# The norms ahead of a product, without GpSimd: a hybrid transformer trunk on one core

## The chip, the cores and the metric

The kernel runs on one core of a Trainium2 chip. Five engines work in parallel, each through its own list of instructions in order: TensorE (PE in the profile, with its weight loads as PEld), VectorE (DVE), ScalarE (ACT), GpSimd (POOL) and SyncE (SP), which here only issues DMAs. The metric is the device time of one execution in microseconds; the median of three runs is 3382.01 us.

## The reference

The program is a two-layer trunk over 1024 latent tokens and 256 context tokens, 1024 channels wide, in f32. Every sub-layer begins with the same step, an RMS norm with a scale and a shift that depend on a conditioning vector, ahead of a matrix product:

```
def rms_norm(x, gain=None):
    y = x32 * lax.rsqrt(jnp.mean(x32 * x32, axis=-1, keepdims=True) + EPS)
...
hx = rms_norm(x) * (1.0 + sc1) + sh1
...
x = x + g1 * mx
x = x + g2 * sq_relu_mlp(rms_norm(x) * (1.0 + sc2) + sh2, w_mlp_in[l], w_mlp_out[l])
```

Layer 0 mixes with an mLSTM and a Hyena convolution side by side, layer 1 with neighbourhood attention over the latent tokens and all context keys. Each mixer has an output product with a gated residual, and each layer ends with a squared-ReLU MLP of width 4096 (the last layer for the latent tokens alone).

## The kernel before

Channels lie on the 128 partitions, in eight blocks of 128, and tokens along the free dimension, in three groups: 512 and 512 latent tokens and 256 context tokens (`GR`). Every f32 product is made of three matmuls on halves: an operand is split into a rounded `hi` and a rest `lo`, and `gemm` adds `hi*hi`, `hi*lo` and `lo*hi` in PSUM (L177 to L179) for each of the eight channel blocks.

A norm has two parts. `norm_sum` squares the eight blocks on ScalarE (L250) into tiles `n`, adds them up, and lets a matmul with a matrix of ones (L266) sum over the partitions, so that each partition holds the sum over all channels. There are two ways to add. With `pre=False`, used for the first norms of the program, the eight squares go through TensorE one after the other. With `pre=True`, used by `norm_group`, they are added in pairs and then as a tree, and one matmul sums the result. After that, `rstd_from` makes the inverse root `r` on ScalarE and VectorE.

`norm_apply` then makes the two halves of the normalised input, block by block. On the usual path VectorE makes `xn = x * (1 + scale) * r`, ScalarE adds the shift and writes the rounded half `hi` (L289), and VectorE writes `lo = xn + shift - hi`. For a block `k` in `ONPOOL` the path is another: GpSimd makes `x * r` into a tile `s`, ScalarE makes `hi` from it (L283) and the unrounded value in place (L284), and GpSimd subtracts them. Two-input instructions of all engines are recorded at the helpers' lines: L96 for a plain `tensor_tensor`, L108 for `scalar_tensor_tensor`.

The tiles come from rings: four buffers under the tag `n2` (shown as `n`; squares, the steps of the inverse root, `r` itself and the usual path's `xn`) and four under `s2` (shown as `s`; partial sums and the GpSimd path's `xn`). A tile that needs a buffer waits for the last reader of the one before.

`norm_group` is called eight times: three groups ahead of the first MLP, where the norm of a group is written behind the residual products of the next one (`LATE2 = 1`); three groups at the end of the first MLP, for the attention's projections; and two groups ahead of the last MLP, between output products of the attention. Six of these have 512 columns and two have 256. Around them, VectorE also takes matmul results out of PSUM into the residual stream (L108), and splits weights (`wl`, L113); ScalarE makes the rounded half of the weights (`wh`, L112).

The order of each engine's list isn't the order of the source. A planner (the Tile framework's scheduler) takes instructions by priority and by its own durations, gives out the buffers, and writes the lists; `pr(...)` raises the priority of some parts.

Of the kernel before, what the change touches and what calls it, by code (L numbers as in the profile page):

```python
# [12 lines left out]
ALU = mybir.AluOpType  # L13
# [14 lines left out]
def kernel(ctx: ExitStack, tc: tile.TileContext, A, out):  # L28
    nc = tc.nc
    V, S, T, G = nc.vector, nc.scalar, nc.tensor, nc.gpsimd  # L30
# [29 lines left out]
    def pr(k):  # L60
        k = HP.get(k, k)
        return ExitStack() if k is None else tc.high_priority(k)
    PS3 = dict(g=3, f=3, m=1, n=1)
    LATE2 = 1
    ONPOOL = (1, 4)
    PS0, PS1 = dict(g=2, f=2, m=1, t=2, q=1), dict(g=4, f=3, m=1)
    PS2 = dict(g=3, f=3, m=1, q=1)
    FS, FH, FM = (0, 0, 0), (0, 1, 0, 1, 0, 1, 0, 2), (3, 4, 4)
# [7 lines left out]
    def pt(shape, tag):  # L76
        cnt[0] += 1
        return psp[0].tile(shape, F32, tag=tag, bufs=psp[1][tag], name=f"ps{tag}_{cnt[0]}")
# [7 lines left out]
    def s2(shape=None):  # L86
        return mk(base, shape or [P, 512], "s2", 4)

    def n2(shape=None):
        return mk(base, shape or [P, 512], "n2", 4)  # L90
# [4 lines left out]
    def tt(o, a, b, op, e=None):  # L95
        return (e or V).tensor_tensor(out=o, in0=a, in1=b, op=op)  # L96

    def add(o, a, b):
        return tt(o, a, b, ALU.add)
# [26 lines left out]
    def rstd_from(ps, n, scale, dst, tmp=None):  # L126

        tmp = tmp or s2
        v = tmp()
        S.activation(v[:, :n], ps, AF.Identity, bias=epsc, scale=scale)  # L130
        y = tmp()
        S.activation(y[:, :n], v[:, :n], AF.Ln)
        S.activation(y[:, :n], y[:, :n], AF.Exp, scale=-0.5)
        mul(dst, y[:, :n], y[:, :n])
        stt(v[:, :n], dst, -0.5, v[:, :n], ALU.mult, ALU.mult)
        stt(dst, v[:, :n], 1.5, y[:, :n], ALU.add, ALU.mult)
# [107 lines left out]
    def norm_sum(xk, n, pre, at=None):  # L244

        ps = pt([P, 512], "m")
        acc = []
        for k in range(8):
            sq = n2()
            S.activation(sq[:, :n], xk(k), AF.Square)  # L250
            if not pre:
                T.matmul(ps[:, :n], ones, sq[:, :n], start=(k == 0), stop=(k == 7))
            elif k % 2 == 0:
                acc.append(sq)
            else:
                a = s2()
                tt(a[:, :n], acc.pop()[:, :n], sq[:, :n], ALU.add, (G, V)[k // 2 % 2])
                acc.append(a)
                if k % 4 == 3:
                    b, a = acc.pop(), acc.pop()  # L260
                    add(a[:, :n], a[:, :n], b[:, :n])
                    acc.append(a)
        if pre:
            add(acc[0][:, :n], acc[0][:, :n], acc[1][:, :n])
            with pr(at):
                T.matmul(ps[:, :n], ones, acc[0][:, :n], start=True, stop=True)  # L266
        r = n2()
        rstd_from(ps[:, :n], n, 1.0 / 1024, r[:, :n], n2)
        return r

    def norm_group(xk, n, l, sub_i, which, hi, lo, at=None):

        with pr("ng"):
            norm_apply(norm_sum(xk, n, True, at), xk, n, l, sub_i, which, hi, lo, True)

    def norm_apply(r, xk, n, l, sub_i, which, hi, lo, pre, ks=range(8)):
        sh, sc = sub_i * 24, sub_i * 24 + 8
        for k in ks:
            b, c = modT[l][:, sh + k, which:which + 1], modT[l][:, sc + k, which:which + 1]
            if k in (ONPOOL if pre else ONP0):  # L280
                xn = s2()
# [773 lines left out]
    with tc.tile_pool(name="hp", bufs=1, side="right") as hp:  # L1055
        hc = {}
        stage = lambda: mk(hp, [P, 512], "st", 1)
        with tc.tile_pool(name="mo", bufs=1, side="right") as mo:
# [13 lines left out]
            def between(u):  # L1072
                if u == -1:
                    hc.update(hyena_consts(hp))
                    mod_part(0, 0, mo, ("wm", 3), "q")
                for v in NS:
                    g = NS.index(v)
                    t0, n = GR[g]
                    which = 0 if t0 < LAT else 1
                    if u == v:  # L1080
                        norms[g] = norm_sum(xload(t0, n), n, False), xload(t0, n)
                    if u in (v, v + 0.5):
                        r, x = norms[g]
                        norm_apply(r, x, n, 0, 0, which, h[0][g], h[1][g], False, range(0, 8)[slice(*NA[u - v])])
                if u > 4 and u == int(u):
                    filler(FS[u - 5], stage)
# [281 lines left out]
```

## Time and profile before

| what | us |
| --- | --- |
| runs (three) | 3377.65, 3382.01, 3385.40 |
| the profiled execution | 3372.65 |
| its span, first to last instruction | 3370.9 |
| PE busy in the span | 3239.5 |
| DVE busy | 2050.1 |
| ACT busy | 1211.5 |
| POOL busy | 272.2 |

The span is what the profile covers; the 1.75 us beside it lie ahead of the first and behind the last recorded instruction. Busy time says how long an engine had an instruction in work, and matmuls are recorded as overlapping, so the PE figure isn't the share of its peak. The norms of `norm_group` lie in three stretches of the span: about 920 to 1010 us (first MLP), 1860 to 1945 us (attention) and 2600 to 2690 us (last MLP). In a timeline row stand the start, the duration, the engine, the line, the operation, output and inputs by the program's names, shapes and count; in brackets the engine's idle time ahead of it and what ended it. In a row of a group stand the total busy time and the mean ns of one, and behind the last bar the idle time ahead of them with its releasers.

### The profile page before, as it was taken

To read this page: it belongs to the slowest core of one execution; us is meant where nothing else is said; L and a number is where in the kernel's file an instruction comes from. 1 tells how busy PE (TensorE), PEld (TensorE's weight loads), DVE (VectorE), ACT (ScalarE), POOL (GpSimd) and SP (SyncE) were. 2 spreads that over 40 slices of the span, in tenths; PEclk is the share of its full clock that TensorE was granted. 3 is DMA by queue.
4 is the path that set the end of the run, shared out by engine and by line. 5 is a ranking of instruction groups with operands and counts; after the bars stand their busy time and mean duration, and the time that the engine had idled before them with its cause. 6 is when DMAs were issued, how large, how long until landed. Compare 5 with 4: busy or idle time off the path is not lost.

```text
span 3370.9 us, 45320 instructions
## 1 busy us (share of the span) xinstructions
PE 3239.5 (96%) x18044; PEld 2640.3 (78%) x18044; DVE 2050.1 (61%) x3673; ACT 1211.5 (36%) x2555; POOL 272.2 (8%) x277
## 2 busy tenths in 40 slices
PE   6889999999989999999999999999999899999999
PEld 4778887778868887878888777777777688888887
DVE  4858997556684454444445776766666654555444
ACT  5742221343441211111121576666664421212121
POOL 0320001011120000000000311111110100000000
PEclk8899999999999999999999999999999999999999
DMA  6432224765522212122110222222224111111111
GB/s 212 153 112 67 80 73 156 231 232 199 193 84 90 75 57 94 57 82 69 51 44 32 72 68 63 65 70 66 70 92 148 61 57 50 51 50 45 49 46 69
DMA packets 140878, 306.12 MB, mean 91 GB/s; under 512 B 12497, under 2 KB 74057, under 8 KB 139258
## 3 DMA queue, kind: packets, MB, share of 16 engines
q1 hardware_dynamic: 131018, 266.60, 24.0%
q0 software_dynamic: 6464, 28.84, 2.7%
q10 hardware_dynamic: 3184, 7.78, 0.7%
q8 instruction: 142, 2.33, 0.3%
q14 instruction: 70, 0.57, 0.1%
HBM read 255.93 MB, written 43.05 MB: 89 GB/s over the span
## 4 chain that ended last, share of the span: by engine, by line
PE 61%; DMA 3%; DVE 3%; ACT 2%; issue 1%; POOL 0%; ACTq 0%; DVEq 0%; POOLq 0%
PE psg L177 10%; PE psg L178 10%; PE psg L179 9%; PE psf L312 8%; PE psf L313 8%; PE psf L314 8%; DMA wm<-in_w_mod 2%; PE psf L1014 2%; PE psm L999 1%; PE psf L978 1%; PE psf L979 1%; DVE n L108 1%; PE psf L1018 1%; PE psm L1006 1%; PE psm L218 1%
## 5 line engine op out<-in xcount | busy, mean ns | idle before, releaser
L177 PE MATMUL psg<-h,wh 128*128 128x512 f32 (+1 forms) x2728 | 1015.2, 372 | 17.5 <-ACT h L289 8.4
L179 PE MATMUL psg<-h,wl 128*128 128x512 f32 (+1 forms) x2728 | 1005.6, 369 | 11.6 <-DVE big L585 5.9
L178 PE MATMUL psg<-h,wh 128*128 128x512 f32 (+1 forms) x2728 | 1012.0, 371 | 3.5 <-DVE h L108 2.6
L177 PEld LDWEIGHTS psg<-h,wh 128*128 128x128 f32 x2728 | 517.0, 190 | 112.0 <-issue 15.9
L179 PEld LDWEIGHTS psg<-h,wl 128*128 128x128 f32 x2728 | 517.1, 190 | 101.4 <-issue 10.8
L178 PEld LDWEIGHTS psg<-h,wh 128*128 128x128 f32 x2728 | 517.4, 190 | 98.0 <-issue 13.6
L108 DVE SCALAR_TENSOR_TENSOR x<-psf,modT,x 128x512 f32<-128x512 f32 (+1 forms) x512 | 347.2, 683 | 222.6 <-PE psf L314 222.3
L313 PE MATMUL psf<-al,w2h 128*128 128x512 f32 (+1 forms) x1280 | 471.8, 369 | 0.3 <-DVE al L113 0.3
L314 PE MATMUL psf<-ah,w2l 128*128 128x512 f32 (+1 forms) x1280 | 471.3, 368 | 0.0
L312 PE MATMUL psf<-ah,w2h 128*128 128x512 f32 (+1 forms) x1280 | 470.0, 370 | 1.2 <-ACT ah L112 1.0
L112 ACT CAST w2h<-w2r 128x1024 fp32r<-128x1024 f32 x64 | 67.3, 1051 | 766.5 <-PE psf L313 594.4
L312 PEld LDWEIGHTS psf<-ah,w2h 128*128 128x128 f32 x1280 | 241.3, 189 | 45.3 <-ACT ah L112 3.9
L313 PEld LDWEIGHTS psf<-al,w2h 128*128 128x128 f32 x1280 | 241.5, 189 | 41.8 <-DVE al L113 1.4
L314 PEld LDWEIGHTS psf<-ah,w2l 128*128 128x128 f32 x1280 | 241.3, 189 | 40.6 <-issue 0.9
L113 DVE TENSOR_TENSOR wl<-wr,wh 128x1024 fp32r<-128x1024 f32 (+1 forms) x123 | 149.6, 1216 | 177.5 <-ACT wh L112 177.0
L112 ACT CAST wh<-wr 128x1024 fp32r<-128x1024 f32 (+2 forms) x144 | 148.5, 1031 | 257.3 <-PE psg L178 194.6
L108 DVE SCALAR_TENSOR_TENSOR rr<-psg,rr 128x512 f32<-128x512 f32 x160 | 101.4, 634 | 180.5 <-ACT rr L301 180.5
L113 DVE TENSOR_TENSOR w2l<-w2r,w2h 128x1024 fp32r<-128x1024 f32 x64 | 78.3, 1223 | 154.1 <-ACT w2h L112 152.4
L301 ACT ACTIVATE rr<-psg 128x512 f32<-128x512 f32 x160 | 88.1, 551 | 197.6 <-PE psg L179 196.3
L112 ACT CAST ah<-rr 128x512 fp32r<-128x512 f32 x160 | 92.3, 578 | 167.9 <-DVE rr L108 167.9
L113 DVE TENSOR_TENSOR al<-rr,ah 128x512 fp32r<-128x512 f32 x160 | 101.8, 637 | 81.7 <-ACT ah L112 81.5
L108 DVE SCALAR_TENSOR_TENSOR h<-psf,modT,h 128x512 f32<-128x512 f32 x128 | 94.2, 748 | 44.0 <-PE psf L314 44.0
(295 smaller groups left out, 4244.7 us busy)
## 6 DMA issues: line engine op xcount, KB each, us to landing
wm<-in_w_mod SPq DMA_DIRECT2D x96, 512.0 KB
wr<-in_w SPq DMA_DIRECT2D x64, 512.0 KB
w2r<-in_w SPq DMA_DIRECT2D x64, 512.0 KB
big<-d SPq DMA_DIRECT2D x39, 640.0 KB
TM<-in_rpbT POOLq DMA_DIRECT2D x64, 384.0 KB, 3.4
wr<-in_w_in SPq DMA_DIRECT2D x29, 512.0 KB
wr<-in_w_qkv SPq DMA_DIRECT2D x24, 512.0 KB
d<-b SPq DMA_DIRECT2D x8, 1280.0 KB
```

What stands on the lines that cost most here:

```text
L108: return V.scalar_tensor_tensor(out=o, in0=a, scalar=s, in1=b, op0=op0, op1=op1)
L112: S.copy(hi, x)
L113: (e or V).tensor_tensor(out=lo, in0=x, in1=hi.bitcast(F32), op=ALU.subtract)
L177: T.matmul(ps[:M, :n], hi[:, k, :M], hh[g][:, k, :n], start=(i == 0), stop=False)
L178: T.matmul(ps[:M, :n], hi[:, k, :M], hl[g][:, k, :n], start=False, stop=False)
L179: T.matmul(ps[:M, :n], lo[:, k, :M], hh[g][:, k, :n], start=False, stop=(i == len(ks) - 1))
L218: T.matmul(ps[0][32 * j:32 * j + 32, c0:c0 + 256], sil[:, k, :], w[:, j], start=(k == 0), stop=(k == 7))
L301: S.activation(r[:, :n], ps[:, :n], AF.Relu)
L312: T.matmul(ps[:, :n], w2h[:, d], ah[g], start=(i == 0), stop=False)
L313: T.matmul(ps[:, :n], w2h[:, d], al[g], start=False, stop=False)
L314: T.matmul(ps[:, :n], w2l[:, d], ah[g], start=False, stop=(i == 1))
L1014: T.matmul(po[64 * hh:64 * hh + 64, rb], Vw[:, rb + j, 64 * hh:64 * hh + 64], pT[hh][0][rb][:, j], start=(j == 0), stop=False)
```

## The change

Two lines. The set of blocks that `norm_apply` gives to GpSimd after a `norm_group` sum becomes empty, so that blocks 1 and 4 take the usual path over VectorE and ScalarE. And of the four pair sums of squares, the first and the third, which GpSimd added, go to VectorE like the others.

```diff
-    ONPOOL = (1, 4)
+    ONPOOL = ()
...
-                tt(a[:, :n], acc.pop()[:, :n], sq[:, :n], ALU.add, (G, V)[k // 2 % 2])
+                tt(a[:, :n], acc.pop()[:, :n], sq[:, :n], ALU.add, V)
```

All eight blocks' `xn` now come from the ring `n2`, where six did; the tiles of the ring `s2` in a norm are the partial sums alone. GpSimd keeps its other work (weight splits in the mLSTM part, copies and loads in the attention).

## The prediction

> **What bounds the kernel now.** First the page's head, then the windows over the stretches with a norm, then the PE timeline of those stretches for waits, then DVE, ACT and POOL beside them.
>
> ```profile
> span 3370.9 us, 45320 instructions
> PE 3239.5 (96%) x18044; PEld 2640.3 (78%) x18044; DVE 2050.1 (61%) x3673; ACT 1211.5 (36%) x2555; POOL 272.2 (8%) x277
> ...
> 945.00:960.00 15.00, 9.98 (x38) 7.04 (x37) 14.72 (x19) 8.69 (x13) 6.89 (x4) 0.77 0.13 46
> 1885.00:1900.00 15.00, 11.31 (x50) 9.06 (x49) 13.28 (x19) 8.74 (x16) 3.01 (x2) 0.89 0.10 36
> 1930.00:1945.00 15.00, 14.53 (x65) 11.55 (x64) 10.38 (x17) 10.71 (x22) 4.78 (x6) 0.83 0.06 15
> 2615.00:2630.00 15.00, 12.11 (x50) 9.43 (x51) 13.42 (x15) 7.47 (x11) 5.96 (x4) 1.00 0.22 71
> ```
>
> A window row gives its start and end, its length, then busy us (and instructions) of PE, PEld, DVE, ACT and POOL, the granted TensorE clock, DMA share and GB/s. PE is busy 96% of the span, so nearly everywhere it is the bound and the edit can't matter. The eight norms ahead of products are the exception. There DVE is busy 14.72 and 13.28 us of 15, PE stands, and behind the longest stands the clock falls to 0.77, 0.89 and 0.83. What PE waits for there:
>
> ```profile
> 951.71 0.50 PE L177 MATMUL psg<-h,wh 128*128 128x512 f32 x1 [4.39 <-ACT h L289]
> 981.66 0.73 PE L177 MATMUL psg<-h,wh 128*128 128x512 f32 x2 [1.48 <-ACT h L289]
> 995.35 0.70 PE L266 MATMUL psm<-s,ones 128*128 128x256 f32 x2 [0.98 <-DVE s L96]
> 1001.67 0.38 PE L177 MATMUL psg<-h,wh 128*128 128x256 f32 x1 [1.62 <-ACT h L289]
> 1890.62 0.61 PE L177 MATMUL psg<-h,wh 128*128 128x512 f32 x1 [3.69 <-ACT wh L112]
> 1929.45 0.79 PE L266 MATMUL psm<-s,ones 128*128 128x256 f32 x1 [3.15 <-DVE s L96]
> 2615.89 1.10 PE L266 MATMUL psm<-s,ones 128*128 128x512 f32 x2 [1.09 <-DVE s L96]
> 2626.02 0.50 PE L179 MATMUL psg<-h,wl 128*128 128x512 f32 x1 [2.00 <-DVE wl L113]
> 2678.52 0.50 PE L177 MATMUL psg<-h,wh 128*128 128x512 f32 x1 [0.88 <-ACT h L289]
> ```
>
> The figure in brackets is PE's idle time and what ended it. These nine make 19.3 us: with the lowered clock behind three of them, that is all there is to win.
>
> **The change part by part.** A 512-wide group now gives POOL six instructions: two of the four pair sums of squares, and for blocks 1 and 4 a product and a subtraction each. All six go to DVE, and ACT loses one of its two activations for each of the two blocks. There are six such groups and two of 256: 36 instructions and 12 small ones. No DMA moves, and POOL's queue only gets shorter.
>
> *What POOL's work costs DVE today.* DVE instructions without POOL beside them (the first row) and with it:
>
> ```profile
> 956.87 2.06 DVE L108 SCALAR_TENSOR_TENSOR n<-x,modT,n 128x512 f32<-128x512 f32 x3
> ...
> 1877.75 4.16 DVE L108 SCALAR_TENSOR_TENSOR n<-x,modT,n 128x512 f32<-128x512 f32 x3
> 1877.86 3.50 POOL L96 TENSOR_TENSOR s<-x,n 128x512 f32<-128x512 f32 x2 [10.11 <-DVE n L108]
> 1882.61 1.66 DVE L108 SCALAR_TENSOR_TENSOR n<-x,modT,n 128x512 f32<-128x512 f32 x1
> 1886.18 1.77 DVE L108 SCALAR_TENSOR_TENSOR h<-n,modT,h 128x512 fp32r<-128x512 f32 x1
> ```
>
> Undisturbed, one takes 2.06 / 3 = 0.69. Beside two POOL products the three take 2.10 more, 1.05 per POOL instruction; the single ones take 0.97 and 1.08 more, each beside one POOL subtraction. So a POOL instruction that meets these DVE instructions holds DVE for about 1.03 us. The groups say the same for the whole kernel:
>
> ```profile
> L96 POOL TENSOR_TENSOR h<-s,h 128x512 fp32r<-128x512 f32 x12 | 19.6, 1637 | 12.8 <-ACT s L284 12.6
> L96 POOL TENSOR_TENSOR s<-n,n 128x512 f32<-128x512 f32 x12 | 18.8, 1563 | 956.7 <-ACT n L250 956.7
> L96 POOL TENSOR_TENSOR s<-n,n 128x256 f32<-128x256 f32 x4 | 3.7, 922 | 9.4 <-ACT n L250 9.4
> ...
> L108 DVE SCALAR_TENSOR_TENSOR h<-n,modT,h 128x512 fp32r<-128x512 f32 x52 | 46.7, 920 | 2.8 <-ACT h L289 2.5
> L108 DVE SCALAR_TENSOR_TENSOR n<-x,modT,n 128x512 f32<-128x512 f32 x30 | 33.5, 1154 | 0.2
> L108 DVE SCALAR_TENSOR_TENSOR n<-h,modT,n 128x512 f32<-128x512 f32 x6 | 7.4, 1274 | 0.0
> L108 DVE SCALAR_TENSOR_TENSOR n<-x,modT,n 128x256 f32<-128x256 f32 x12 | 8.3, 732 | 0.1
> L96 DVE TENSOR_TENSOR s<-n,n 128x512 f32<-128x512 f32 x12 | 8.2, 686 | 3.2 <-ACT n L250 3.2
> L96 DVE TENSOR_TENSOR s<-n,n 128x256 f32<-128x256 f32 x4 | 1.9, 468 | 2.3 <-ACT n L250 2.3
> ```
>
> The 36 `n` of 512 take 33.5 + 7.4 = 40.9 us where 36 x 0.69 = 24.8 would do, the 52 `h` 46.7 in place of 35.9: 27 us held. Sixteen of those `h` belong to the first norms, so it is at most 27 / 24 = 1.1 per POOL instruction of the blocks.
>
> *The blocks on DVE.* Per 512-wide group four holds of 1.03 go and four instructions of 0.69 come: -1.36. I take -1.3 for the four groups ahead of the attention and the second MLP, where DVE is never waiting. Ahead of the first MLP less is held:
>
> ```profile
> 947.89 3.52 DVE L108 SCALAR_TENSOR_TENSOR n<-x,modT,n 128x512 f32<-128x512 f32 x3
> 948.56 0.81 ACT L283 ACTIVATE h<-s,modT 128x512 fp32r<-128x512 f32 x1 [1.36 <-POOL s L96]
> 950.95 0.71 ACT L289 ACTIVATE h<-n,modT 128x512 fp32r<-128x512 f32 x1
> ```
>
> Here the products hold DVE 1.46 and not 2.1; I take -0.7 for each of these two groups. With 256 columns the 12 `n` lose 8.3 - 12 x 0.47 = 2.7 us, and eight instructions of 0.47 come, 3.8, while the subtractions' holds go too: nothing either way. Sum 4 x 1.3 + 2 x 0.7 = 6.6 us. It lies on the path: the last halves of `h` come off DVE, PE's columns end with them, and at 1890.62 the cast of the attention's first weights stands behind the last `h` in ACT's list. The rows of ACT show a second effect: it takes POOL's block 1 and 4 ahead of block 0, so the first `h` comes out at 951.66, while DVE's product from 947.89 could give it at about 947.9 + 0.7 + 0.7 = 949.3. I count that as nothing, because DVE's total still decides when the column ends. ACT's shorter list is worth nothing either, ACT being at 8.69 of 15.
>
> *The sums on DVE.* The add on a chain falls from 1.56 to 0.69 us (0.92 to 0.47 in the small groups). What PE's three waits for the sum rest on, and an eviction of a residual with an add behind it:
>
> ```profile
> L250 ACT ACTIVATE n<-x 128x256 f32<-128x256 f32 x16 | 5.6, 406 | 1.6 <-POOL s L96 1.6
> ...
> 2609.81 2.50 POOL L96 TENSOR_TENSOR s<-n,n 128x512 f32<-128x512 f32 x1 [2.29 <-ACT n L250]
> ...
> 931.23 0.75 DVE L108 SCALAR_TENSOR_TENSOR x<-psg,modT,x 128x512 f32<-128x512 f32 x1 [0.61 <-PE psg L1169]
> 931.90 0.68 DVE L96 TENSOR_TENSOR s<-n,n 128x512 f32<-128x512 f32 x1
> ```
>
> At 995.35 one add is less slow, -0.5. At 1929.45 two are, because ACT's squares wait for POOL's add to give a buffer back (1.6 us in the first row): -0.9. At 2615.89 one POOL add took 2.50, so the whole 1.09 can go. That is -2.5. The cost is 12 x 0.69 + 4 x 0.47 = 10.2 us more on DVE. What covers it is the 0.61 us that DVE stands between two evictions of a residual: an add of 0.68 fills that slot, eight evictions leave eight slots, and a group has seven adds. So nothing, from 0 up to 10.2 if the cover is gone.
>
> [...]
>
> *The clock.* Behind stands of 4.39, 3.69 and 3.15 it is below 1.00; in the window with the stand of 2.00 it is 1.00. After the edit the second is 3.69 - 1.3 = 2.4 and the third 3.15 - 0.9 = 2.25, nearer to 2.00. Their windows lost 15 x 0.11 = 1.65 and 15 x 0.17 = 2.55 us of clock. I take half, -2.1, from 0 to -4.2. The first stretch gives nothing, since `h` comes no faster than DVE makes it.
>
> [...]
>
> *The order.* Tile's planner writes every engine's list from its own durations and these change, so PE, ACT and DVE get other lists. The trace of before can't show them. The bounds come from its rows: one stand of 4.39 less, or two such stands more (9). I take +3, as a weight split planned behind DVE's longer norm costs what 2626.02 shows, 2.00, once or twice.
>
> Sum: -6.6 - 2.5 - 2.1 + 3 = -8.2 us against the profiled execution's 3372.65 (span 3370.9, 1.75 around it): 3364.4. The median shown, 3382.01, is 9.4 above that execution, so 3373.8; I say 3374.
>
> **The rivals.**
>
> *The gain is eaten* (about 3381). The list is planned anew, and what DVE wins is lost to weight splits and evictions that now stand behind it. For it: 2626.02, where PE waits for `wl` and not for the norm. Against: 1929.45 and 2615.89 wait for the sum itself. 9.1 of gains, 2 x 4 of such waits: -1.
>
> *DVE's slots are full* (slower). If the pair sums don't fit between the evictions, the 10.2 us stand on the path. The place is the tail of each residual product, where PSUM banks come free only through DVE; it decides once more than one add falls into one slot of 1.36 us (0.75 and 0.61), as where DVE was already at 13.42 of 15 around the second MLP's norm. With the blocks' 6.6 lost as well, since three `n` buffers must carry eight blocks instead of six, it is +10.2, and with the waits won back, -2.5, +7.7: 3390. Against: one square leaves ACT per eviction, so adds can't come faster than slots; and a buffer cycles in 0.75 + 0.71 + 0.75 = 2.2 us, three of them faster than DVE's 1.38 per block.
>
> *The clock stays up everywhere* (3364). All three windows' 15 x (0.23 + 0.11 + 0.17) = 7.7 us come back and the lists don't get worse: -9.1 - 7.7 = -17. For it: the gaps all shrink. Against: the first stretch is DVE's.
>
> That the edit does nothing is no rival: the norms' three POOL groups lie in DVE's busiest windows.
>
> **How the numbers follow.** About 0.2% (6.8 us) is what a measurement here can tell from no change. Forecast (3366 to 3375): 0.44. Gain eaten (3375 to 3388.8): 0.31. Slots full (over 3388.8): 0.18. Clock up (under 3366): 0.07. So faster 0.51, same 0.31, slower 0.18. The forecast's own range is 3366 to 3375; for 8 in 10 I go from 3360 to 3388, which takes in most of the eaten gain and the clock's bound and leaves out the full slots and little below.
>
> **What would show it.** In the profile after: POOL has no instruction in the norms; the `n` and `h` groups of 512 fall from 1154 and 920 ns to about 690 to 750, which carries the 6.6; DVE's total stays within some us of 2050 (+10.2 of adds and +20 of blocks against 27 to 30 held); the stands at 1890, 1929 and 2616 shrink to about 2.4, 2.3 and none; the windows around them show a clock near 1.00. Wrong: if the `n` stay at 1.1 us, POOL wasn't what held DVE; if they fall and the stands stay, DVE's time wasn't the path; if new PE waits of 2 us and more for `wl` or for evictions appear, the order decided.

## The result

The changed kernel takes 3358.6 us (median of 6 runs, 3353.4 to 3359.8), the kernel before 3383.6 on the same chip (median of 6, 3377.7 to 3386.2). The ratio is 0.9929, with a 95% interval from 0.9919 to 0.9939: about 24 us, or 0.7%, faster. In a second comparison, with 5 and 18 runs, it was 0.9936 (0.9923 to 0.9949), 22 us. The forecast was -8.2 us and 3374, with a range of its own from 3366 to 3375 and one for 8 in 10 from 3360 to 3388: the direction was right, the size was a third of the real one, and the time lies just below the wider range.

The head of the profile after: the same columns as before.

```profile
span 3358.0 us, 45267 instructions
PE 3233.0 (96%) x18044; PEld 2641.5 (79%) x18044; DVE 2045.8 (61%) x3721; ACT 1200.9 (36%) x2539; POOL 203.3 (6%) x229
```

DVE has taken over 48 instructions and is busy 4.3 us *less* (2050.1 before). The groups of DVE by form say where that comes from (busy us, mean ns, then the idle time ahead of them):

```profile
L108 DVE SCALAR_TENSOR_TENSOR h<-n,modT,h 128x512 fp32r<-128x512 f32 x64 | 45.6, 752 | 1.7 <-ACT h L289 1.4
L108 DVE SCALAR_TENSOR_TENSOR n<-x,modT,n 128x512 f32<-128x512 f32 x40 | 27.8, 746 | 0.1
...
L108 DVE SCALAR_TENSOR_TENSOR n<-h,modT,n 128x512 f32<-128x512 f32 x8 | 5.6, 744 | 0.0
```

The products fell from 1154 and 1274 ns to 746 and 744, the subtractions from 920 to 752: 112 instructions now take 79.0 us where 88 took 87.6. The windows over the stretches with norms, in the order PE, PEld, DVE, ACT, POOL, clock, DMA share, GB/s:

```profile
945.00:960.00 15.00, 10.04 (x63) 8.33 (x61) 13.57 (x24) 7.58 (x10) 0.00 (x0) 0.93 0.11 36
955.00:970.00 15.00, 5.84 (x17) 4.30 (x18) 15.00 (x23) 10.18 (x16) 0.00 (x0) 0.66 0.15 44
1885.00:1900.00 15.00, 13.76 (x78) 11.35 (x77) 14.66 (x24) 10.14 (x17) 0.00 (x0) 1.00 0.12 35
1930.00:1945.00 15.00, 11.50 (x50) 8.56 (x51) 12.79 (x25) 11.31 (x22) 0.66 (x1) 0.89 0.12 36
2615.00:2630.00 15.00, 14.54 (x63) 11.40 (x62) 14.87 (x21) 7.84 (x11) 0.00 (x0) 1.00 0.25 88
```

DVE is at least as full as before (12.8 to 15 of 15, before 10.4 to 14.7), now with its own work. The clock is 1.00 at 1885 and 2615 and 0.89 at 1930, but 0.66 from 955 on. PE's waits there, from its timeline:

```profile
956.17 0.50 PE L177 MATMUL psg<-h,wh 128*128 128x512 f32 x1 [2.12 <-ACT h L289]
965.16 0.80 PE L179 MATMUL psg<-h,wl 128*128 128x512 f32 x1 [7.27 <-DVE wl L113]
1890.66 0.47 PE L177 MATMUL psg<-h,wh 128*128 128x512 f32 x1 [0.94 <-ACT h L289]
1931.77 0.39 PE L177 MATMUL psg<-h,wh 128*128 128x256 f32 x1 [1.82 <-ACT h L289]
2619.02 0.50 PE L179 MATMUL psg<-h,wl 128*128 128x512 f32 x1 [0.31 <-DVE wl L113]
```

The stand of 3.69 at the attention's first product is 0.94, the 3.15 for the sum is gone (a wait of 1.82 for `h` stands near its place), the 2.00 for `wl` is 0.31. One stand is new and the longest of all: 7.27 us for `wl` in the first MLP, because the planner put that split behind fourteen of the norm's sixteen block instructions.

**Three stretches, measured by their own length.** The two kernels have the same instructions up to the first product of the residual, and yet their traces reach it at different times:

```profile
917.75 0.40 PE L1167 MATMUL psg<-h,wh 128*128 128x512 f32 x1
```

is the kernel before, and

```profile
924.32 0.40 PE L1167 MATMUL psg<-h,wh 128*128 128x512 f32 x1
...
1086.89 1.05 ACT L112 CAST w2h<-w2r 128x1024 fp32r<-128x1024 f32 x1 [24.10 <-PE psf L313]
1853.39 1.05 ACT L112 CAST w2h<-w2r 128x1024 fp32r<-128x1024 f32 x1 [4.83 <-DMA w2r<-in_w]
2574.72 1.04 ACT L112 CAST w2h<-w2r 128x1024 fp32r<-128x1024 f32 x1
2743.27 1.05 ACT L112 CAST w2h<-w2r 128x1024 fp32r<-128x1024 f32 x1 [17.51 <-PE psf L313]
```

the changed one. So ends of spans are no measure here. The rows mark three stretches by the same events in every kernel: from that first product to the fifth cast of `w2h` (first MLP), from the 32nd to the 33rd (attention), and from there to the 37th (last MLP). For each run below, from its own trace, in us:

```
                        first MLP  attention  last MLP    sum    DVE busy in all
before                    168.2      729.1      176.6   1073.8      2050.1
before, second trace      167.1      728.3      177.7   1073.1      2051.1
changed                   162.6      721.3      168.6   1052.5      2045.8
changed, second trace     162.5      719.2      168.6   1050.4      2048.9
e2  sums only             163.1      729.1      175.6   1067.8      2055.7
e3  blocks only           164.3      726.3      169.6   1060.2      2043.2
e4  holds put back        173.7      736.0      176.9   1086.6      2075.9
e5  split first, 300      161.4      721.6      169.6   1052.6      2047.5
e6  split first, 600      161.4      719.5      168.5   1049.4      2046.9
e7  split on GpSimd       161.4      719.5      171.8   1052.7      2046.1
e9  one block             168.0      730.2      175.6   1073.8      2051.3
e10 blocks 3 and 6        169.3      724.8      176.9   1071.0      2055.1
e11 holds early           165.0      729.6      171.5   1066.1      2062.2
e12 holds late            165.3      725.1      173.5   1064.0      2059.7
e13 short GpSimd          160.4      716.3      170.0   1046.7      2025.2
e14 short DVE             157.6      721.4      169.4   1048.4      2036.7
```

Two traces of one kernel agree within 1 to 2 us in the sum. (The trace of e14 is of its slowest execution, 3360.3 us at a granted clock of 0.941.) The change gains 5 us ahead of the first MLP (forecast 1.9), 7 to 10 ahead of the attention (5.6 with the clock) and 8 to 9 ahead of the last MLP (3.7): 22 in all, which is what the medians say.

### The profile page after: what moved, and what is told of

Its sections match the earlier page's. It is cut to its first block, busy times and chain, and to the rows that moved or that the text cites. A ratio compares the mean times of both kernels' runs of the same rounds, so it can differ in the third digit from the quotient of the medians.

```text
span 3358.0 us, 45267 instructions
## 1 busy us (share of the span) xinstructions
PE 3233.0 (96%) x18044; PEld 2641.5 (79%) x18044; DVE 2045.8 (61%) x3721; ACT 1200.9 (36%) x2539; POOL 203.3 (6%) x229
## 4 chain that ended last, share of the span: by engine, by line
PE 66%; DVE 4%; DMA 4%; ACT 2%; issue 1%; POOL 0%; SPq 0%; ACTq 0%; DVEq 0%
PE psg L177 11%; PE psg L178 11%; PE psg L179 11%; PE psf L313 8%; PE psf L312 8%; PE psf L314 8%; DMA wm<-in_w_mod 3%; PE psf L1014 2%; PE psm L999 1%; PE psf L978 1%; PE psf L979 1%; DVE n L108 1%; PE psf L1018 1%; PE psm L1006 1%; PE psm L218 1%; PE psn L902 1%
## 5 line engine op out<-in xcount | busy, mean ns | idle before, releaser
L177 PE MATMUL psg<-h,wh 128*128 128x512 f32 (+1 forms) x2728 | 1014.4, 372 | 11.5 <-ACT h L289 5.3
```

The costliest lines, as they stand in the source:

```text
L177: T.matmul(ps[:M, :n], hi[:, k, :M], hh[g][:, k, :n], start=(i == 0), stop=False)
```

## The experiments

**e1, the changed kernel once more**, beside e2 to e4 on one chip.

> The changed kernel once more, beside the three others on one chip, so that they can be compared with it and not with the kernel before alone. A theory called holds says that the gain is DVE time given back (24 POOL instructions of the blocks of 512 columns at 1.03 us each, and POOL's adds); a theory called lists says that the gain is the other order that the planner writes, and the round trip through POOL that is gone. Both expect what was measured, a ratio of 0.992 to 0.994, about 24 us less. If the part of the trace ahead of the norms (up to 920 us, where both kernels have the same instructions) moves by several us against the earlier execution, then the differences between executions ahead of the norms are chance, and the stages have to be compared by their own lengths.

Measured: 0.9936 (0.9923 to 0.9949), 3359.8 us. The first product of the residual came at 922.23, so the part ahead of the norms does move by chance.

**e2, only the sums.**

```diff
-                tt(a[:, :n], acc.pop()[:, :n], sq[:, :n], ALU.add, (G, V)[k // 2 % 2])
+                tt(a[:, :n], acc.pop()[:, :n], sq[:, :n], ALU.add, V)
```

> Only the pair sums move to DVE; POOL keeps blocks 1 and 4. The step of the prediction for the sums: -2.5 us against the kernel before (0.9993). The rival of full slots: +2.5 to +10, because DVE then carries 10.2 us more with all the holds of the blocks still there. Lists: anything between -6 and +6, to be seen in PE's waits; in the traces of before and after the wait for the sum was 0.98, 3.15 and 1.09 us, so a gain of more than 6 us would have to come from the new order.

Measured: 0.9984 (0.9974 to 0.9995), -5.4 us. On balance the ten microseconds of adds did not lengthen the time, as they would have by the rival of full slots, which is out; that the slots between the evictions of the residual cover all of them fits this, but isn't shown by itself. DVE's total rose by 5.1 (mean of both traces of before: 2050.6), not by the 10.2 of added work: the sums' own holds came off. The gain is twice what the three waits for the sum gave, and nearly all of it lies in the first MLP's stretch, where these waits had put 0.5; the attention's stretch, where they had put 0.9, stayed as long as it was.

**e3, only the blocks.**

```diff
-    ONPOOL = (1, 4)
+    ONPOOL = ()
```

> Only blocks 1 and 4 move to DVE; POOL keeps two of four pair sums. The steps of the prediction for the blocks and the clock: -6.6 - 2.1 = -8.7 us against the kernel before (0.9974). Holds, as the traces of after now stand (three stages shorter by 3.6, 7.7 and 7.9 us): most of the 24, -16 to -21 us, and the sums make up the rest. Lists: DVE's list of the first MLP differs from the changed kernel's at few places and has the weight split behind all of the norm's blocks as well, so the same new wait of about 7 us at 965 us.

Measured: 0.9959 (0.9947 to 0.9972), -13.9 us; the forecast for blocks and clock was -8.7. What the sums do when they stay on GpSimd stands in DVE's groups of this run:

```profile
L108 DVE SCALAR_TENSOR_TENSOR h<-n,modT,h 128x512 fp32r<-128x512 f32 x64 | 47.9, 791 | 1.4 <-ACT h L289 1.1
...
L96 DVE TENSOR_TENSOR s<-s,s 128x512 f32<-128x512 f32 x18 | 13.3, 739 | 0.9
L96 DVE TENSOR_TENSOR s<-n,n 128x512 f32<-128x512 f32 x12 | 9.3, 777 | 2.1 <-ACT n L250 2.1
```

Against 752 for `h` in the changed kernel and 686 for undisturbed adds: the sums of the next group fall beside the last blocks of this one and hold them. Moving the sums is worth 5.4 us alone and about 8 once the blocks are gone (0.9959 to 0.9936); in DVE's total these holds come to about 6 us here (2043.2 + 10.2 of adds against a mean of 2047.4 in the changed kernel).

**e4, the holds put back and nothing else.** GpSimd works into scratch tiles; every other engine has the changed kernel's list, instruction for instruction.

```diff
+    def extra(x, r, n):
+        z = s2(); tt(z[:, :n], x, r[:, :n], ALU.mult, G); tt(z[:, :n], z[:, :n], x, ALU.subtract, G)
...
-            xn = n2()
+            xn = n2(); pre and k in (1, 4) and extra(xk(k), r, n)
```

> The changed kernel with the holds put back and nothing else: for blocks 1 and 4 POOL computes a product and a subtraction into scratch tiles that nobody reads (32 instructions, 24 of them on 512 columns); DVE still computes all eight blocks. The instruction lists of PE, DVE, ACT and the DMA queue are the same as in the changed kernel, instruction for instruction, and no engine waits for POOL's work but for a scratch tile. Holds: the n and h groups of DVE go back from 746 and 752 ns to 1000 or more, DVE's total rises by 24 x 1.03 = 25 us, and since the norms' blocks are on the path the time rises by 15 to 20 us above the changed kernel (ratio to the kernel before 0.997 to 0.999). Lists: POOL's work is on nobody's path, so at most 4 us above the changed kernel (0.993 to 0.994).

Measured: 1.0028 (1.0018 to 1.0039), 3391.7 us: 31 us slower than the changed kernel, more than the 15 to 20 expected, and slower than the kernel before. DVE's total rose by 27 to 30. A norm of this run ahead of the attention, DVE and then GpSimd:

```profile
1892.41 4.16 DVE L108 SCALAR_TENSOR_TENSOR n<-x,modT,n 128x512 f32<-128x512 f32 x3
...
1896.49 4.14 DVE L108 SCALAR_TENSOR_TENSOR h<-n,modT,h 128x512 fp32r<-128x512 f32 x3
...
1892.52 3.50 POOL L96 TENSOR_TENSOR s<-x,n 128x512 f32<-128x512 f32 x2 [874.95 <-DVE n L108]
1895.98 3.44 POOL L96 TENSOR_TENSOR s<-s,x 128x512 f32<-128x512 f32 x2
```

and the same six instructions of DVE in the changed kernel:

```profile
1880.55 2.08 DVE L108 SCALAR_TENSOR_TENSOR n<-x,modT,n 128x512 f32<-128x512 f32 x3
...
1882.54 2.07 DVE L108 SCALAR_TENSOR_TENSOR h<-n,modT,h 128x512 fp32r<-128x512 f32 x3
```

2.08 and 2.07 us more for two GpSimd instructions each: 1.04 us a hold, which is the prediction's 1.03. In the three stretches no wait of another engine ends with that work, so the 31 us are the holds and what they bring along (the mean granted clock is 0.985 in place of 0.989). With these lists, a microsecond of DVE's time in a norm is about a microsecond of the kernel's.

**e5 and e6, the first weight split ahead of the norm.** m0 is the priority of the first two up-projection weights.

```diff
-    HP = dict(..., m0=150, ...)
+    HP = dict(..., m0=300, ...)      # e6: m0=600
```

> The changed kernel with one more edit: the priority m0 of the first two up-projection weights of an MLP is 300 in place of 150, so that the planner puts their splits on DVE ahead of the norm's last blocks (in the changed kernel the split stands behind fourteen instructions of the norm, and PE stands 7.27 us for it at 965 us). If that stand is a price of its own (theory price: the new order costs 3.6 us, the lost time at 50 us into the first MLP's stretch was 15.1 in place of 11.5), the stand goes, the stretch of the first MLP gets 2 to 4 us shorter and the ratio to the kernel before falls from 0.9936 to about 0.9925. Theory no price: PE has the same work waiting later, finds it ready and catches up, so that the stretch keeps its length within 1 us and the ratio stays at 0.993 to 0.994.

> The same with m0 at 600: the first split stands two evictions of the residual earlier, its DMA is issued earlier too. Theory price: like the run with 300, a ratio of about 0.9925. Theory no price: 0.993 to 0.994. Both allow a loss of 1 to 2 us where the split, 1.4 us of DVE, now stands ahead of residual evictions and of the norm's last step (0.994 to 0.9945).

Measured: 0.9928 (0.9915 to 0.9942) and 0.9935 (0.9923 to 0.9948): not to be told from the changed kernel. The stand of 7.27 us is gone in both, and the first MLP's stretch is 1.1 us shorter, as the table shows. But other waits came in its place. In e5 DVE makes two splits ahead of the norm's products; PE waits 4.39 us for the first `h` and not 2.12, and 1.45 for an activation. In e6 PE waits 2.22, 2.12 and 1.70 us in that stretch. So 1.1 us is the net of the two orders, and the price of the stand alone isn't measured. Neither theory's number was met exactly, "no price" was nearer.

**e7, that split on GpSimd.**

```diff
-    E1, E2, E3, E4, E5 = None, None, None, None, None
+    E1, E2, E3, E4, E5 = None, G, None, None, None
```

> The changed kernel with the low parts of the first two up-projection weights of each MLP computed by GpSimd (one subtraction of 1024 columns each) and not by DVE. DVE loses 4 instructions of about 1.4 us, and PE's stand of 7.27 us for the split goes or shrinks, if GpSimd finishes in time. Theory holds: a GpSimd instruction of 1024 columns beside the norm's blocks holds DVE twice as long as one of 512, about 2.1 us, so the n and h beside it take 2.1 us more and the gain of 1.4 + 3.6 us shrinks to 0 to 3 (ratio 0.9930 to 0.9936). Theory free: GpSimd costs nothing there and the ratio falls to 0.992.

Measured: 0.9941 (0.9928 to 0.9955), above what both theories gave (0.9930 to 0.9936, and 0.992), though the interval takes in the first. The first MLP's stretch is 1.1 us shorter than the changed kernel's, the last MLP's 3.2 longer. The hold has the size of GpSimd's instruction, as the timeline of DVE and of GpSimd in the first norm shows:

```profile
957.33 0.74 DVE L108 SCALAR_TENSOR_TENSOR n<-x,modT,n 128x512 f32<-128x512 f32 x1
958.03 2.83 DVE L108 SCALAR_TENSOR_TENSOR h<-n,modT,h 128x512 fp32r<-128x512 f32 x1
...
957.45 2.85 POOL L113 TENSOR_TENSOR wl<-wr,wh 128x1024 fp32r<-128x1024 f32 x1 [4.68 <-ACT wh L112]
```

1024 columns hold one `h` for 2.83 - 0.74 = 2.09 us, twice the hold of 512.

**e8, the kernel before once more**, for a second trace.

> The kernel before, unchanged, for a second trace of it. The profiled execution of before had reached the first residual product at 917.75 us, those of five other kernels, with the same instructions up to there, at 919.4 to 926.7. If that is chance of the execution, this one lies anywhere from 917 to 927, and the three stretches with norms keep their lengths within 1 us (168.15 us from there to the fifth w2h, 729.06 us for the stretch of the attention, 176.55 us for the last MLP's).

Measured: the first product of the residual at 926.31 and not 917.75, the stretches at 167.1, 728.3 and 177.7: the first and the last miss the bound of 1 us by 0.1 each, in opposite directions, and the sum differs by 0.7.

**e9, one block on GpSimd; e10, two later blocks**, both with all sums on DVE.

```diff
-    ONPOOL = ()
+    ONPOOL = (1,)      # e10: (3, 6)
```

> The changed kernel, but GpSimd keeps block 1 of the eight (block 4 and all sums on DVE): half the holds of the run with only the sums moved (ratio there 0.9984; changed kernel 0.9936). Holds as a price per instruction: half of the way, 0.9960, about -13 us, the groups of 512 columns half as much longer, 12.0 us in place of 11.3 and 12.8. A theory called threshold says that one POOL block is enough for PE's stands (its chain through ACT and back is as long as with two), so the ratio stays near the one with two blocks, 0.997 to 0.9985.

> The sums on DVE, GpSimd keeps two blocks, but 3 and 6 in place of 1 and 4, so that ACT can take block 0 first: the same holds as in the run with only the sums moved (0.9984), another head. The prediction counted the head (the first h comes 0.7 to 1.3 us later where ACT takes GpSimd's blocks ahead of block 0) as nothing: then the ratio stays at 0.998 to 0.999. Theory head: the first h comes 1.5 us after the first product in place of 2.1 to 2.75, in six groups, and PE's columns start that much earlier: -3 to -6 us, 0.9965 to 0.9975.

Measured: 0.9987 (0.9976 to 0.9999) and 0.9992 (0.9982 to 1.0001). One block costs as much as two: "threshold" is what the numbers say, although DVE's time is almost that of the changed kernel (2051.3 against 2045.8 and 2048.9). What can be seen is the order. ScalarE, DVE and PE's wait ahead of the attention in e9:

```profile
1896.07 1.32 ACT L289 ACTIVATE h<-n,modT 128x512 fp32r<-128x512 f32 x2
1897.30 1.03 ACT L112 CAST wh<-wr 128x1024 fp32r<-128x1024 f32 x1
1898.38 1.01 DVE L108 SCALAR_TENSOR_TENSOR rr<-psg,rr 128x512 f32<-128x512 f32 x2
...
1899.21 0.47 PE L177 MATMUL psg<-h,wh 128*128 128x512 f32 x1 [3.58 <-DVE rr L108]
```

In the changed kernel the cast of the weights and DVE's reading of the last up-projection out of PSUM (`rr`) stand ahead of the last blocks' `h`, here both stand behind them, and it is `rr` that ended PE's wait:

```profile
1887.53 1.04 ACT L112 CAST wh<-wr 128x1024 fp32r<-128x1024 f32 x1
1889.28 1.38 ACT L289 ACTIVATE h<-n,modT 128x512 fp32r<-128x512 f32 x2 [0.71 <-DVE n L108]
1889.83 0.68 DVE L108 SCALAR_TENSOR_TENSOR rr<-psg,rr 128x512 f32<-128x512 f32 x1
1890.43 1.40 DVE L108 SCALAR_TENSOR_TENSOR h<-n,modT,h 128x512 fp32r<-128x512 f32 x2
```

PE's stand is 3.58 in place of 0.94. In the first MLP's stretch e9 and e10 both have a stand for `wl` as the changed kernel does (6.30 and 7.70 us) and longer norms behind it. That the order alone makes the difference isn't shown. e10 gave no verdict on the head: its first `h` came 2.1 to 2.8 us after the first product in five of six groups, as with blocks 1 and 4, because the holds delay DVE's first products and ScalarE still took GpSimd's block first.

**e11 and e12, half of the holds, early or late.** In e11 GpSimd multiplies blocks 1 and 4 into scratch tiles; in e12 it does two instructions that can start only after block 4's `h`. The other engines' lists are again the changed kernel's.

```diff
+        z = s2(); tt(z[:, :n], x, r[:, :n], ALU.mult, G)      # e11: extra, called for k in (1, 4) as in e4
+            pre and k == 4 and extra(xk(k), hi[:, k, :].bitcast(F32), n)      # e12: e4's extra, called behind the subtraction
```

> The changed kernel with half of the holds put back, at the head of each norm: GpSimd multiplies blocks 1 and 4 into scratch tiles that nobody reads, two instructions a group that run beside DVE's first three products. The lists of PE, DVE, ACT and the DMA queue are those of the changed kernel. All four holds a group cost 32 us (ratio 1.0028 against 0.9936). If each hold costs the same wherever it falls (theory price per hold): half, about +16 us above the changed kernel, a ratio of 0.998 to 0.999, and the same in the run with late holds. If PE's columns start with the first h and the head decides (theory head): the first h comes 1.1 us later, in series with everything behind it; more than the late holds by 5 us and more, 0.999 to 1.000.

> The changed kernel with two holds a group put back at the end of each norm: GpSimd multiplies and subtracts into a scratch tile that nobody reads, from block 4's h on, beside DVE's last instructions. The same lists, the same number of GpSimd instructions as with the early holds. Price per hold: about +16 us, a ratio of 0.998 to 0.999. Theory head: the first half of the columns runs as in the changed kernel and only the last blocks come 2 us later; less than the early holds, +5 to +11 us, 0.9955 to 0.997.

Measured: 0.9982 (0.9973 to 0.9990) and 0.9966 (0.9952 to 0.9979), 16 and 10 us above the changed kernel's 0.9936; DVE's total rose by 13 to 16 and by 11 to 14. The ratio to DVE's time is about 1 for both, the intervals overlap, and half of the holds cost half. The two differ by 5 us, the least that the theory of the head asked for, but they differ in DVE's time as well, by 2.5; that leaves about 3 us for the head, which these runs can't tell from nothing. Nor did they move it much: block 0's `h`, with which PE's columns begin, came 13.7 us after DVE's first products in e11, summed over the eight norms, and 11.5 in e12.

**e13, GpSimd's work cut short in the kernel before.** GpSimd keeps its two blocks, ScalarE its two activations for each, the lists are nearly those of before, but GpSimd's instructions have 64 columns. ScalarE's two activations repeat these over the block, the second straight into `lo`, so the right values of the other columns of blocks 1 and 4 are left out.

```diff
-                tt(xn[:, :n], xk(k), r[:, :n], ALU.mult, G)
+                tt(xn[:, :64], xk(k)[:, :64], r[:, :64], ALU.mult, G)
...
-                tt(lo[:, k, :], xn[:, :n], hi[:, k, :].bitcast(F32), ALU.subtract, G)
+                tt(lo[:, k, :64], lo[:, k, :64].bitcast(F32), hi[:, k, :64].bitcast(F32), ALU.subtract, G)
```

> The kernel before, with GpSimd's products and subtractions of blocks 1 and 4 on 64 of the columns only (the rest of these two blocks is filled from those 64 by ScalarE's two activations, so the blocks' values are not the reference's). GpSimd still takes both blocks, ScalarE still does two activations for each, DVE still six blocks, and the instruction lists are nearly those of before (64 lines of PE's differ, against 299 between before and the changed kernel). The holds shrink from 1.03 to about 0.13 us each. Theory old holds at full price: DVE loses 24 x 0.9 = 22 us and the time falls with it, 20 to 28 us, a ratio of 0.992 to 0.994, as fast as the changed kernel or faster. Theory order and round trip: these stay, so the ratio stays at 0.997 or above (10 us at most).

Measured: 0.9922 (0.9910 to 0.9934), -26 us. DVE's groups and a norm:

```profile
L108 DVE SCALAR_TENSOR_TENSOR h<-n,modT,h 128x512 fp32r<-128x512 f32 x52 | 39.0, 776 | 2.7 <-ACT h L289 2.6
L108 DVE SCALAR_TENSOR_TENSOR n<-x,modT,n 128x512 f32<-128x512 f32 x30 | 21.9, 774 | 0.2
...
1878.98 2.21 DVE L108 SCALAR_TENSOR_TENSOR n<-x,modT,n 128x512 f32<-128x512 f32 x3
...
1879.09 1.56 POOL L96 TENSOR_TENSOR s<-x,n 128x64 f32<-128x64 f32 x2 [10.10 <-DVE n L108]
```

Two GpSimd products of 64 columns hold three DVE products for 0.14 us in place of 2.1. DVE's total falls by 25.4 and the time by 26. So in nearly the old order, with the round trip through GpSimd still there, short GpSimd instructions were worth as much as the whole change. This run doesn't separate the holds from the shorter round trip: a GpSimd product that takes 0.8 us and not 1.75 also hands its block to ScalarE sooner.

**e14, the work that came to DVE cut short in the changed kernel.**

```diff
-            stt(xn[:, :n], xk(k), c, r[:, :n], ALU.mult, ALU.mult)
+            stt(xn[:, :q], xk(k)[:, :q], c, r[:, :q], ALU.mult, ALU.mult)      # q = 64 for blocks 1 and 4
...
-            stt(lo[:, k, :], xn[:, :n], b, hi[:, k, :].bitcast(F32), ALU.add, ALU.subtract)
+            stt(lo[:, k, :q], xn[:, :q], b, hi[:, k, :q].bitcast(F32), ALU.add, ALU.subtract)
```

> The changed kernel with DVE's product and subtraction of blocks 1 and 4 on 64 of the columns only (the rest of these two blocks filled by two activations of ScalarE, so the blocks' values are not the reference's): the work that came to DVE, 24 instructions of 512 columns and 8 of 256, is nearly taken away again, about 24 x 0.54 + 8 x 0.3 = 15 us of DVE. The planner's lists change here. If DVE's time in the norms is on the path at 1.1 us for 1: 17 us below the changed kernel, a ratio of 0.988 to 0.990. If that work is hidden: at most 5 us below, 0.992 to 0.9936.

Measured: 0.9911 (0.9898 to 0.9925), 6 to 9 us below the changed kernel (by its two ratios) for the 15 us of work estimated there: between the two theories. In its trace DVE's total fell by 9 to 12 us and not by 15, and the three stretches by 2 to 4, so some of that work may be hidden. The lists differ here, so this is the weakest of the prices.

## Why the prediction was right and wrong

**The hold: right, and it is the larger part of the cause.** 1.03 us for each GpSimd instruction of 512 columns; e4 measures 1.04, e7 2.09 for 1024, e13 0.07 for 64. What was to show it came: the groups at 744 to 752 ns, a DVE total within some us of 2050. The stands at 1890 and 1929 shrank further than forecast (0.94 and 1.82 for 2.4 and 2.3). The sign that the order decided, a new wait for `wl` of 2 us and more, came too.

**The blocks (-6.6): the DVE time was right, the time was not.** e3 lowers DVE's total by 7.4, and the kernel's time by 13.9. Measured from a group's first product, on either engine, to its last subtraction on DVE, the two groups of 512 columns ahead of the attention were nearly as forecast at -1.3 (12.79 to 11.28 us and 12.52 to 10.91). Those ahead of the first MLP, for which I took -0.7, fell more (13.66 to 11.82 and 12.99 to 11.29): GpSimd's start ahead of DVE's (0.63 and 0.45 us) is gone, and with it a wait of 0.28 for ScalarE's `h` in the first and one eviction between the blocks in the second. The last group ahead of the last MLP fell by 2.4 (13.67 to 11.28), and the group of 256 columns ahead of the first MLP, taken as nothing, by 1.0 (8.10 to 7.09). The other group of 256 grew (7.22 to 7.56), and so did the first group ahead of the last MLP (16.47 to 17.14). The last MLP's stretch still got 8 us shorter, and PE's wait of 2.00 for `wl` fell to 0.31: there the norm's length on DVE wasn't what decided.

**The sums (-2.5): the term was too small.** e2 gives -5.4 alone, and the step from e3 to the changed kernel about -8. I had counted PE's three waits for the sum and, by my estimate, no hold to win back from the adds. That is out: GpSimd's adds also run beside the blocks and adds of DVE and hold them, for 5 to 6 us in all (in e2 DVE grew by 5.1 us for 10.2 of work; in e3 `h` takes 791 ns against 752 and the adds 739 and 777 against 686). The evictions show no hold (before, the twelve evictions of 512 columns beside a GpSimd product or add take 746 ns on average, all 408 of them 750). That the cost of the adds is nothing fits what was measured.

**The order (+3), with the head and ScalarE's list counted as nothing: this step failed, and it is the largest part of the miss.** An account in DVE's time, in which a microsecond of blocks counts 1 (e4, e11, e12) and the 10.2 us of adds count nothing (taken from e2, whose rest is 0 for that reason):

```
                 DVE's change   without the adds   measured     rest
e2  sums only        +5.1            -5.1            -5.4         0
e13 short GpSimd    -25.4           -25.4           -26.4        -1
e3  blocks only      -7.4            -7.4           -13.9        -6
changed              -3.3           -13.5           -21.6        -8
e4  holds back      +25.3           +15.1            +9.5        -6
e11 holds early     +11.6            +1.4            -6.1        -7
e12 holds late       +9.1            -1.1           -11.5       -10
e14 short DVE       -13.9           -24.1           -30.1        -6
e9  one block        +0.7            -9.5            -4.4        +5
e10 blocks 3 and 6   +4.5            -5.7            -2.7        +3
```

(DVE against 2050.6, the mean of both traces of before; changed: the mean of its two; measured from the ratios, with about 4 us of uncertainty each.) The forecast's terms for blocks and sums, 9.1 us together, answer to the 13.5. What is left had +0.9 in the forecast (order +3, clock -2.1) and is -8: 9 of the 13 us by which it missed the 21.6. The order was argued from one side, since a weight split behind a longer norm had to cost. That split did come, with the longest stand of the trace, and taking it away again in e5 and e6 shortened the stretch by 1.1 us on balance. What might be gained elsewhere was not in the sum at all. The term's own range, -4.4 to +9, was too narrow for the -8.

Where the -8 comes from is not settled. ScalarE's shorter list isn't it, as far as the one trace of e14 goes: there ScalarE does two activations for both blocks again, and the rest is -6. In the table the rest is -6 to -10 in every kernel whose products take no block from GpSimd (e5 to e7, reckoned alike, come to -5 to -11), and -1 to +5 in every one that does (e2, e9, e10, e13). A rival for the order is therefore the head, which the forecast counted as nothing: PE's columns begin with block 0, and in most norms ScalarE takes GpSimd's block ahead of it. Summed over the eight norms, block 0's `h` was ready 27.5 us after the first product of either engine in the kernel before and 11.1 in the changed one. In e2, e9 and e10 it was 24 to 26, in e13 17.6, in e3 and e14 11, in e4, e11 and e12 11.5 to 14. Four waits of PE in the trace of before end with this `h` (4.39, 1.48, 1.62 and 0.88 us), in the changed kernel two (2.12 and 1.82). The rest follows these figures, but the planner's lists changed along with them, and no run moved the head alone.

**"All there is to win" (19.3 us and the clock): wrong.** The forecast added nine stands and the lowered clock behind three of them. Behind a long stand PE's loss does go on inside its busy time. After the stand of 4.39 in e2, the timeline of PE has

```profile
953.28 0.79 PE L177 MATMUL psg<-h,wh 128*128 128x512 f32 x1 [4.39 <-ACT h L289]
...
957.35 0.63 PE L177 MATMUL psg<-h,wh 128*128 128x512 f32 x1
957.78 0.63 PE L178 MATMUL psg<-h,wh 128*128 128x512 f32 x1
958.21 0.60 PE L179 MATMUL psg<-h,wl 128*128 128x512 f32 x1
...
959.34 0.39 PE L177 MATMUL psg<-h,wh 128*128 128x512 f32 x1
959.57 0.39 PE L178 MATMUL psg<-h,wh 128*128 128x512 f32 x1
```

that is, starts 0.43 apart, and 0.23 apart only two microseconds later; these rows hold no idle time and the engine counts as busy. This much goes with the granted clock, which the forecast had counted: in the trace of before, behind its own stand of 4.39, the clock is 0.50 from 953 to 959, where starts are 0.43 apart (955.79 to 958.35), and 1.00 from 960 on, where they are 0.23 apart. But if every matmul is taken as its columns / 512 x 0.227 us (the spacing of undisturbed ones: before, nine steps from 963.83 to 965.87) and the rest of a stretch as lost, the first 170, 130 and 150 us of the three stretches lose about 67 us before and 47 after. Of the 67, PE stands idle for 33, and so for 14 us in waits that the nine leave out (one of 1.55 for `wl` at 2610.61, which the change leaves at 1.51, and many short ones). The lowered clock is worth 10, and the other 23 lie inside PE's busy time. How much of the 47 could still be won isn't shown.

**The clock (-2.1): not confirmed.** The window from 1885 came back from 0.89 to 1.00, the one from 1930 went from 0.83 to 0.89, which would make 2.5 us. But the traces are shifted against each other, and fixed windows don't compare them: the second trace of before has 1.00 from 1885, the second of the changed kernel 0.77 from 1930. Over the whole of the three stretches, one minus the clock times the length is 13.7 and 10.2 us in the two traces of before, and 10.2 in both of the changed kernel. That is no more than two traces of one kernel differ.

**The rivals.** "The gain is eaten" expected the new wait for `wl` and got it, but not its price. "Slots full" is out by e2. "The clock stays up everywhere" (3364) came nearest in time, by luck: in the first stretch the clock still falls, to 0.66.

**The basis: harmless.** The profiled execution of before lay 9.4 us under the median; the second trace shows that 8.6 us of this came ahead of the norms, by chance.

## What to carry to other kernels

Before work is given to GpSimd beside VectorE, price the hold and not the work: here a two-input instruction of 512 columns took VectorE 0.69 us to do itself and cost it 1.04 us when GpSimd did it, most of it on the path, so that the relief was a loss from the first block on. VectorE's total doesn't show it: it changed by 3 us while the kernel gained 22, because 10 us of adds that lengthened nothing came along. Ask also which block the next product begins with, and when that one is ready. Where a planner writes the lists, give the order a term with both signs, as wide as what other splits of the same work show (here the rest was -11 to +5), and judge a new stand by the length of its stretch and not by its own.

## What the runs showed of the hardware that was not expected

The hold grows with GpSimd's columns: 0.07 us for 64, about 0.5 for 256 (e4's norms of 256 columns took 1.9 to 2.2 us longer for four), 1.04 for 512, 2.09 for 1024.

The clock fell without a long stand. In the second trace of the changed kernel, ahead of the attention, no wait of PE is longer than 1.84 us, and yet in windows of 5 us

```profile
1930.00:1935.00 5.00, 2.52 (x13) 1.65 (x11) 4.67 (x12) 3.04 (x7) 0.00 (x0) 0.98 0.00 0
1935.00:1940.00 5.00, 4.87 (x15) 3.54 (x16) 4.17 (x9) 2.67 (x7) 0.00 (x0) 0.50 0.10 22
1940.00:1945.00 5.00, 4.54 (x21) 3.23 (x21) 3.15 (x4) 4.47 (x9) 0.61 (x1) 0.83 0.23 86
```

the granted clock is 0.50 right after a window in which PE was busy only half of the time. The prediction took the length of a single stand as what decides; here waits of 1.84, 0.26 and 0.44 us within that window stood ahead of the fall.
